# A decoder trunk in split fp32: the seven products of a block in another sequence, and the first six steps as plain fp32

## The chip, the core and the metric

The kernel runs on one core of a Trainium2 chip. Its time is the device time of one execution in microseconds. TensorE (PE) multiplies and writes to PSUM, eight banks of 512 fp32 columns on 128 partitions; weight loads into it have a row of their own (PEld). VectorE (DVE), ScalarE (ACT) and GpSimd (POOL) do the elementwise work; SyncE (SP) and POOL issue the DMAs.

## The reference

A stream of 256 tokens by 1024 goes through two layers. Each has a SwiGLU FFN of half weight, an attention and a second such FFN. The first attention is stick-breaking with 16 heads, the second a sliding window with sinks on shared keys and values. Four FFNs in all make most of the arithmetic:

```
def swiglu(x, w_in, w_out):
    gate, up = jnp.split(x @ w_in, 2, axis=-1)
    return (jax.nn.silu(gate) * up) @ w_out

h = h + 0.5 * swiglu(rms_norm(h, ffn1_norm[layer]), ffn1_w_in[layer], ffn1_w_out[layer])
...
h = h + 0.5 * swiglu(rms_norm(h, ffn2_norm[layer]), ffn2_w_in[layer], ffn2_w_out[layer])
```

with w_in 1024 x 5632 and w_out 2816 x 1024, all fp32.

## The kernel before

**Split products.** A weight comes from HBM as fp32 into one of five `raw` buffers of 1 MB. `split` (L394) makes two operands of the faster type fp32r of it: ACT casts it into `w_hi`, and DVE subtracts that from `raw` into `w_lo`, each in two halves. x is kept split the same way as `xh` and `xl` (both in the tile `xT`). One step of k (`step`, L423) is then three products of 512 columns into one PSUM bank: x_hi by w_hi, x_lo by w_hi, x_hi by w_lo.

**Blocks of an FFN.** The 2816 columns are cut into blocks of 512 (`plain`, "p", or `strassen`, "s") and one of 256 (`narrow`, "h"). The first FFN is p, h, s, s, s, s; the other three are h and five s. A plain block takes both token tiles t by gate and up by 1024 of k, 32 steps. A Strassen block computes the 2 x 2 problem (two tiles by gate and up, the two halves of k) with seven products of four steps in place of eight, in three banks a, d and b (`strassen`, L713). Its raw weights are r11 (gate, first half of k), r12 (up, first half), r22 (up, second half), r21 (gate, second half), and sums of them that DVE makes in place or that POOL adds by DMA. In the order of the code:

1. a: tile 0 by r11; ACT copies a into b (L751), where b goes on from it. In the first Strassen block of the last three FFNs ACT copies a into the SBUF tile s1 instead.
2. d: first operand sum by r11 + r12; ACT copies d into the SBUF tile p5 (`stage`, L735; the profile calls it p).
3. d: fourth operand sum by r22, added to what is in d.
4. b: tile 0 by r21; then silu into s1.
5. a: second operand sum by r11 + r12 + r22 of step 2's buffer; ACT copies a into u2 (the profile's u). DVE then makes s1 * (u2 + d), and PE turns the result (`turn`, L641).
6. a: third operand sum by r12 + r22; DVE adds a to p5.
7. a: tile 1 by r11 + gate's second half; silu, times p5, and a second turn.

Products 3 and 6 write the bank that ACT has just copied, so they wait for that copy. Between 6 and 7 stands the product of the block before with its w_out (`out`).

**What sets the order.** Nothing runs in the order of the code. `Plan` (L118) collects tasks with an engine, an estimated duration and dependencies, and lists them engine by engine with a priority queue: what is ready in its estimate and has the lowest priority goes next. So steps of another product or of `out` are drawn in where a step would wait. Each engine then works its own list strictly in that order. A freed `raw` buffer goes to the back of a queue (`Slots`), and the next load takes the front one and waits for the last reader of it.

**The opening.** x of tile 0 comes in two halves, then the first gate weight in four pieces of 256 KB, x of tile 1, and further weights. PE transposes x (`first_operand`, L1339), DVE multiplies it by the norm's gain in PSUM (L1342), ACT and DVE split it into xh and xl. PE runs warm-up products on a constant until the first split weights are there. Block p takes each half weight for both tiles in turn.

## Time and profile before

| | us |
|---|---|
| median of 3 runs | 913.63 |
| lowest and highest | 913.60, 913.98 |
| the profiled execution | 913.31 |
| its span, first to last instruction | 911.5 |
| PE busy | 899.3 |
| DVE busy | 818.2 |
| ACT busy | 649.6 |

In a timeline row stand start, time taken, engine, line, operation, output and inputs, shapes, the number of merged instructions, and in brackets the engine's idle time before them with what ended it. In a row of stretches stand, for PE, PEld, DVE, ACT and POOL, the busy time with the number of instructions, then the granted PE clock, the DMA engines' mean share and GB/s. A row of waits has the total in us, the number of times and the longest. Ends of products are modelled and overlap, so what a product costs is read from start to start.

### The profile page before, as it was taken

How to read it: one execution, taken by the hardware profiler on the slowest of the kernel's cores; microseconds unless marked ns; L12 is line 12 of the kernel's file. 1: busy time of each engine (PE TensorE's matmuls, PEld its weight loads, DVE VectorE, ACT ScalarE, POOL GpSimd, SP SyncE). 2: the span in 40 equal slices, each digit the busy share in tenths (PEclk: the TensorE clock that was granted, in tenths of full speed). 3: DMA queues.
4: the chain of work that ended last, by engine and by line, in shares of the span. 5: the costliest groups of instructions: out<-in, count | busy, mean ns of one | idle time of the engine just before them, and what ended most of it. 6: DMA issues, size and time to landing. Idle time of an engine off the chain costs nothing.

```text
span 911.5 us, 11855 instructions
## 1 busy us (share of the span) xinstructions
PE 899.3 (99%) x4446; PEld 743.7 (82%) x4446; DVE 818.2 (90%) x981; ACT 649.6 (71%) x925; POOL 65.5 (7%) x71
## 2 busy tenths in 40 slices
PE   9999999999999999999999999999999999999997
PEld 7888888888888878888888878888897777888886
DVE  7989999787967999999969999999689799999986
ACT  6857668677986865876778767667867677686663
POOL 1010101000000100110000101010000001010100
PEclk9999999999999999999999999999999999999999
DMA  9887999996853499999884999899853349998971
GB/s 335 311 203 216 306 268 242 311 246 186 264 184 126 106 260 284 236 280 303 251 269 135 251 279 276 256 326 234 298 180 116 94 94 273 293 258 268 335 209 47
DMA packets 107306, 214.44 MB, mean 235 GB/s; under 512 B 6256, under 2 KB 27760, under 8 KB 107248
## 3 DMA queue, kind: packets, MB, share of 16 engines
q1 hardware_dynamic: 85184, 170.49, 52.3%
q0 software_dynamic: 21648, 42.99, 27.2%
q8 instruction: 35, 0.57, 0.2%
q10 hardware_dynamic: 416, 0.20, 0.1%
q14 instruction: 23, 0.19, 0.1%
HBM read 212.62 MB, written 1.05 MB: 234 GB/s over the span
## 4 chain that ended last, share of the span: by engine, by line
PE 81%; DVE 15%; issue 2%; ACT 2%; POOL 0%; DVEq 0%; POOLq 0%; ACTq 0%
PE ps L283 77%; DVE w_lo L406 6%; PE ps L641 2%; DVE raw L575 1%; PE ps L455 1%; ACT w_hi L404 1%; DVE S_l L545 1%; DVE s L551 1%; DVE xT L462 1%; DVE w_lo L1115 1%; PE ps L1281 0%; DVE xs L1379 0%; DVE hN L532 0%; DVE aT_l L462 0%; DVE e L1273 0%
## 5 line engine op out<-in xcount | busy, mean ns | idle before, releaser
L406 DVE TENSOR_TENSOR w_lo<-raw,w_hi 128x1024 fp32r<-128x1024 f32 x432 | 509.3, 1221 | 30.3 <-ACT w_hi L404 28.5
L404 ACT CAST w_hi<-raw 128x1024 fp32r<-128x1024 f32 x432 | 430.1, 1050 | 96.7 <-DVE raw L575 41.1
L283 PE MATMUL ps<-w_hi,xT 128*128 128x512 f32 (+1 forms) x800 | 233.3, 375 | 0.0
L283 PEld LDWEIGHTS ps<-w_hi,xT 128*128 128x128 f32 x800 | 144.7, 188 | 25.9 <-DVE xT L462 0.2
L283 PE MATMUL ps<-w_lo,xT 128*128 128x512 f32 (+1 forms) x400 | 149.2, 373 | 0.3 <-DVE w_lo L406 0.3
L283 PE MATMUL ps<-w_hi,aT_h 128*128 128x512 f32 x354 | 139.9, 395 | 0.0
L283 PE MATMUL ps<-w_lo,aT_h 128*128 128x512 f32 x354 | 137.7, 389 | 0.0
L283 PE MATMUL ps<-w_hi,aT_l 128*128 128x512 f32 x354 | 137.5, 388 | 0.0
L283 PE MATMUL ps<-w_hi,S_h 128*128 128x512 f32 x320 | 126.9, 396 | 1.5 <-ACT p L735 1.5
L283 PE MATMUL ps<-w_lo,S_h 128*128 128x512 f32 x320 | 124.9, 390 | 0.3 <-DVE w_lo L406 0.3
L283 PE MATMUL ps<-w_hi,S_l 128*128 128x512 f32 x320 | 124.7, 390 | 0.0
L575 DVE TENSOR_TENSOR raw<-raw 128x1024 f32<-128x1024 f32 x78 | 93.7, 1221 | 0.2
L283 PEld LDWEIGHTS ps<-w_lo,xT 128*128 128x128 f32 x400 | 75.3, 188 | 14.4 <-DVE w_lo L406 1.1
L580 POOL DMA_DIRECT2D raw<-in_ffn_w_in_dram x38 | 48.1, 1267 | 516.8 <-DVE w_lo L406 218.0
L283 PEld LDWEIGHTS ps<-w_lo,aT_h 128*128 128x128 f32 x354 | 66.5, 188 | 13.9
L283 PEld LDWEIGHTS ps<-w_hi,aT_l 128*128 128x128 f32 x354 | 66.6, 188 | 12.9
L283 PEld LDWEIGHTS ps<-w_hi,aT_h 128*128 128x128 f32 x354 | 66.5, 188 | 12.8
L283 PEld LDWEIGHTS ps<-w_hi,S_h 128*128 128x128 f32 x320 | 60.1, 188 | 15.3 <-ACT p L735 3.0
L283 PEld LDWEIGHTS ps<-w_lo,S_h 128*128 128x128 f32 x320 | 60.1, 188 | 13.5 <-DVE w_lo L406 0.7
L283 PEld LDWEIGHTS ps<-w_hi,S_l 128*128 128x128 f32 x320 | 60.2, 188 | 11.6
L461 ACT CAST aT_h<-ps 128x512 fp32r<-128x512 f32 (+1 forms) x48 | 26.4, 549 | 55.1 <-PE ps L641 53.6
L283 PE MATMUL ps<-xT,w_hi 128*128 128x512 f32 (+1 forms) x136 | 46.8, 393 | 0.0
(176 smaller groups left out, 918.5 us busy)
## 6 DMA issues: line engine op xcount, KB each, us to landing
raw<-in_ffn_w_in_dram SPq DMA_DIRECT2D x76, 1024.0 KB, 7.8
raw<-in_ffn_w_out_dram SPq DMA_DIRECT2D x44, 1024.0 KB, 6.6
raw<-in_ffn_w_in_dram POOLq DMA_DIRECT2D x38, 1024.0 KB, 9.6
raw<-in_sb_w_qkv_dram SPq DMA_DIRECT2D x12, 1024.0 KB, 9.4
raw<-in_ffn_w_in_dram SPq DMA_DIRECT2D x16, 512.0 KB, 6.7
raw<-in_ffn_w_in_dram SPq DMA_DIRECT2D x16, 256.0 KB, 5.4
raw<-in_sb_w_o_dram SPq DMA_DIRECT2D x4, 1024.0 KB, 5.2
raw<-in_swa_w_q_dram SPq DMA_DIRECT2D x4, 1024.0 KB, 9.3
```

Of the source, the lines that this page charges most:

```text
L283: PE.matmul(ps, lhsT=lhsT, rhs=rhs, start=start, stop=stop, skip_group_check=True)
L404: T("ACT", act(m), lambda sl=sl: ACT.copy(out=flat(hi)[:, sl], in_=flat(raw)[:, sl]), r=[(raw, i) for i in rs] + first, w=[(hi, i) for i i ...
L406: T("DVE", dve(m), lambda sl=sl: DVE.tensor_sub(out=flat(lo)[:, sl], in0=flat(raw)[:, sl], in1=flat(hi)[:, sl].bitcast(F32)), r=[(raw, i) ...
L455: PE.matmul(bank.ap[:, i * P:(i + 1) * P], lhsT=s, rhs=ident, start=i == 0, stop=True, is_transpose=True, skip_group_check=True)
L461: T("ACT", act(n), lambda: ACT.copy(out=hi[2](), in_=src()), r=B(bank), w=[hi[0:2]])
L462: T("DVE", dve(n), lambda: DVE.tensor_sub(out=lo[2](), in0=src(), in1=hi[2]().bitcast(F32)), r=B(bank) + [hi[0:2]], w=[lo[0:2]])
L545: T("DVE", dve(512), lambda: DVE.tensor_sub(out=SL.ap[:, i].rearrange("p a b -> p (a b)"), in0=b.ap, in1=SH.ap[:, i].rearrange("p a b -> p ...
L551: T("DVE", dve(512), lambda: DVE.scalar_tensor_tensor(out=dst.ap, in0=x_.ap, scalar=sign, in1=y_.ap, op0=ALU.mult, op1=ALU.subtract), r=B( ...
L575: T("DVE", dve(m), lambda sl=sl: DVE.tensor_add(out=flat(dst)[:, sl], in0=flat(dst)[:, sl], in1=flat(src)[:, sl]), r=[(src, k) for k in ks ...
L580: T("POOL", 1500, lambda: nc.gpsimd.dma_start(out=dst.ap, in_=src, accum_op=ALU.add), w=[(dst, 0), (dst, 1)], prio=plan.pos - LOADS, lat=5 ...
L641: PE.transpose(out=tr.ap[:, i * P:(i + 1) * P], in_=m.ap[:, i * P:(i + 1) * P], identity=ident)
L1115: T("DVE", dve(512), lambda k=k, g_=g_: DVE.scalar_tensor_tensor(out=lo.ap[:, k], in0=raw.ap[:, k], scalar=g_(), in1=hi.ap[:, k].bitcast(F ...
```

## The change

*The sequence in a Strassen block* (`ORD = "6t"`). Product 3 (`third`) moves behind product 5 and its copy u2. Product 4 (`second`) thereby follows product 2 and its copy p5. In the first Strassen block of the last three FFNs `second` moves further ahead, right behind product 1. The first turn stands ahead of product 6 as before.

*The opening.* For tile 0, the first six of gate's eight steps of k (`DIRECT = 6`) are one product each of unsplit fp32 operands: the raw weight and `x_f`, an SBUF tile into which DVE now writes the multiplied x. xh and xl are made from x_f too, and ACT copies x_f back into the bank. The weights of block p are still split, for tile 1 and the other steps, and now in four quarters each (`FINES`, `split_fine`). Block p now goes tile by tile (`FIRST_T`): gate and up of tile 0, then of tile 1. Warm-up tasks of two products fall from 20 to 10 (`WARM`), and the second tile's x gets a later place (`POSX`).

```diff
+DIRECT = 6
+FINES = (4, 4, 4, 4)
+FIRST_T = True
+ORD = "6t"
-WARM = 14
+WARM = 9
-POSX = (-20000.0, -6000.0)
+POSX = (-20000.0, 0.0)
...
+    def split_fine(raw, prio):
+        a, b = raw.ab
+        hi, lo = WP.get([P, a, b], F32R, "w_hi"), WP.get([P, a, b], F32R, "w_lo")
+        n = a // raw.fine
+        for c in range(0, a, n):
...
+            T("ACT", act(n * b), lambda sl=sl: ACT.copy(out=flat(hi)[:, sl], in_=flat(raw)[:, sl]),
...
+            T("DVE", dve(n * b), lambda sl=sl: DVE.tensor_sub(out=flat(lo)[:, sl], in0=flat(raw)[:, sl],
...
+    def direct(bank, raw, kk, xf, first, last):
+        def run():
+            mm(bank.ap, xf.ap[:, kk], raw.ap[:, kk], first, last)
+
+        dense(4 * 512 / 2.4 + 20, run, r=[(raw, kk), (xf, 0)], w=B(bank))
...
                     for i in range(2):
+                        if first and t == 0 and 4 * i < DIRECT:
+                            raw = load([(slice(0, 512), col(0, i, c))], 4, 512, cut)
+                            gw[i] = split(raw)
+                            for kk in range(4):
+                                if 4 * i + kk < DIRECT:
+                                    direct(b, raw, kk, plainly[i], i == kk == 0, i == 1 and kk == 3)
+                                else:
+                                    step(b, gw[i], kk, of_x(0, 4 * i + kk), i == kk == 0, i == 1 and kk == 3)
+                            RAW.put(raw)
+                            STG.put(plainly[i])
+                            continue
                         gate(t, i, b)
...
+            early = n == 1 and blocks[0] != "p"
+
+            def second(c11):
+                product(b, r21, lambda kk: of_x(0, 4 + kk), not c11, True)
+                RAW.put(r21)
...
+            def third():
+                product(d, r22, of_s(3), False, True)
+                RAW.put(r22)
+
             product(a, r11, lambda kk: of_x(0, kk), True, False)
...
+            if early:
+                second(False)
             add(r11, r12)
             product(d, r11, of_s(0), True, False)
             p5 = stage(d, "p5")
...
-            product(d, r22, of_s(3), False, True)
-            RAW.put(r22)
-            product(b, r21, lambda kk: of_x(0, 4 + kk), not c11, True)
-            RAW.put(r21)
...
+            if not early:
+                second(C11)
...
             product(a, r11, of_s(1), False, False)
             fetch(r11, col(0, 1, c))
             u2 = stage(a, "u2")
+            if ORD[0] == "6":
+                third()
             plus(u2, d)
...
-                outs[n] = plain(n, cols_[n], n == 0 and not first, 4 if first and n == 0 else 2)
+                outs[n] = plain(n, cols_[n], n == 0 and (FIRST_T or not first), 4 if first and n == 0 else 2)
...
+        if t == 0 and 4 * j < DIRECT:
+            plainly[j] = xf = STG.get([P, 4, P], F32, "x_f")
+            T("DVE", dve(512), lambda: DVE.tensor_mul(
+                out=xf.ap, in0=quarters(bank), in1=gin[:, j].unsqueeze(2).to_broadcast([P, 4, P])), r=B(gc, bank), w=B(xf))
...
+            copy_act(lambda: quarters(bank), lambda: xf.ap, 512, B(xf), B(bank), prio=0.0)
+            return
```

On PE, at the start of the program, these rows stood behind the last warm-ups (hN is x, its transposes go to ps; w_hi_178 and w_lo_202 are the first gate weight):

```order
L283 LDWEIGHTS warm_71
L283 MATMUL ps_66<-warm_71 128x256
L455 MATMUL ps_66<-ident_68,hN_63 128x128 x4
L283 MATMUL ps_66<-w_hi_178,xT_158 128x512 x2
L283 MATMUL ps_66<-w_lo_202,xT_158 128x512
L455 MATMUL ps_66<-ident_68,hN_63 128x128 x4
L283 MATMUL ps_66<-w_hi_178,xT_158 128x512 x2
```

And now, from the last of four warm-ups on (raw_113 and raw_185 are the two halves of k of the gate weight, w_hi_170 and w_lo_176 the split of the first):

```order
L288 LDWEIGHTS warm_71
L288 MATMUL ps_66<-warm_71 128x256
L288 MATMUL ps_66<-raw_113,x_f_152 128x512 x4
L491 MATMUL ps_66<-ident_68,hN_63 128x128 x4
L288 LDWEIGHTS warm_71
L288 MATMUL ps_66<-warm_71 128x256
L288 LDWEIGHTS warm_71
L288 MATMUL ps_66<-warm_71 128x256
L491 MATMUL ps_66<-ident_68,hN_63 128x128 x4
L288 MATMUL ps_66<-raw_185,x_f_167 128x512 x2
L288 MATMUL ps_66<-w_hi_170,xT_163 128x512 x2
L288 MATMUL ps_66<-w_lo_176,xT_163 128x512
```

The plain products stand ahead of the second tile's transposes; 22 warm-ups that stood before the first product are gone from there, and three split steps of tile 1 follow the sixth plain product before tile 0's last two steps.

On PE, in the second Strassen block of the third FFN, these rows stood where d's first product (w_hi_4234) ends and d's second (w_hi_4263, the split of r22) begins:

```order
L283 MATMUL ps_66<-w_hi_4234,S_h_4019 128x512
L283 MATMUL ps_66<-w_hi_4234,S_l_4035 128x512
L283 MATMUL ps_66<-w_lo_4251,S_h_4019 128x512
L283 MATMUL ps_66<-w_hi_4263,S_h_4019 128x512
L283 MATMUL ps_66<-w_hi_4263,S_l_4035 128x512
L283 MATMUL ps_66<-w_lo_4280,S_h_4019 128x512
L641 MATMUL ps_66<-ident_68,m_4298 128x128 x4
```

And now (w_hi_4236 is d's first product, w_hi_4268 b's, w_hi_4303 a's second, w_hi_4284 d's second):

```order
L288 MATMUL ps_66<-w_hi_4236,S_h_4025 128x512
L288 MATMUL ps_66<-w_hi_4236,S_l_4032 128x512
L288 MATMUL ps_66<-w_lo_4250,S_h_4025 128x512
L288 MATMUL ps_66<-w_hi_4268,xT_163 128x512 x2
L288 MATMUL ps_66<-w_lo_4282,xT_163 128x512
...
L288 MATMUL ps_66<-w_hi_4303,S_h_4025 128x512
L288 MATMUL ps_66<-w_hi_4303,S_l_4032 128x512
L288 MATMUL ps_66<-w_lo_4319,S_h_4025 128x512
...
L288 MATMUL ps_66<-w_hi_4284,S_h_4025 128x512
```

Four steps of b and two of a stand where nothing stood; steps of a's second and d's second product then alternate by twos.

More of the change, by code (lines that the diff above doesn't have):

```diff
@@ L47 @@
 BOOST = 10000.0
+DIRECT = 6
+FINES = (4, 4, 4, 4)
+AFTER = 4
+FIRST_T = True
 C11 = True
@@ L101, in __init__ @@
         self.slot = None
-        self.by_halves = False
+        self.by_halves = self.fine = False
     @property
@@ L385, in load @@
         raw.ab, raw.cut = (a, b), cut
+        raw.fine, raw.after = 2, {}
+        if cut == 4:
+            raw.fine = FINES[fines[0]]
+            if fines[0] == 0:
+                raw.after = {k: [(xh, (0, 0))] for k in range(AFTER, 4)}
+            fines[0] += 1
         return raw
+    fines = [0]
     def flat(buf):
@@ L395, in split @@
         a, b = raw.ab
+        if raw.cut == 4:
+            return split_fine(raw, prio)
         hi, lo = WP.get([P, a, b], F32R, "w_hi"), WP.get([P, a, b], F32R, "w_lo")
@@ L409, in split @@
         return hi, lo
+    def split_fine(raw, prio):
[3 more added lines that the diff above has]
+        for c in range(0, a, n):
+            ks, at_ = range(c, c + n), [(buf, k) for buf in (hi,) for k in range(c, c + n)]
+            sl = slice(c * b, (c + n) * b)
+            T("ACT", act(n * b), lambda sl=sl: ACT.copy(out=flat(hi)[:, sl], in_=flat(raw)[:, sl]),
+              r=[(raw, k) for k in ks] + raw.after.get(c, []), w=[(hi, k) for k in ks], prio=prio)
+            T("DVE", dve(n * b), lambda sl=sl: DVE.tensor_sub(out=flat(lo)[:, sl], in0=flat(raw)[:, sl],
+                                                              in1=flat(hi)[:, sl].bitcast(F32)),
+              r=[(raw, k) for k in ks] + [(hi, k) for k in ks], w=[(lo, k) for k in ks], prio=prio)
+        hi.fine = lo.fine = True
+        return hi, lo
     def weight(parts, a, b, cut=2, keep=False):
@@ L425, in step @@
         hi, lo = w
-        piece = kk // 2 if piece is None else piece
+        piece = kk if hi.fine else kk // 2 if piece is None else piece
         def run():
@@ L744, in mul_less @@
                   r=r + (B(roots[t][1]) if late else []), w=w, lat=LAT["DVE"] + TM)
+            early = n == 1 and blocks[0] != "p"
+            def second(c11):
+                product(b, r21, lambda kk: of_x(0, 4 + kk), not c11, True)
+                RAW.put(r21)
+                if c11:
+                    silu(lambda: s1.ap, lambda: b.ap, B(b), B(s1), 0)
+                else:
+                    plus(s1, b)
+                    silu(lambda: s1.ap, lambda: s1.ap, [], B(s1), 0)
+            def third():
+                product(d, r22, of_s(3), False, True)
+                RAW.put(r22)
             product(a, r11, lambda kk: of_x(0, kk), True, False)
-            c11 = C11 and (n != 1 or blocks[0] == "p" or C11_0)
-            if c11:
+            if C11 and not early:
                 T("ACT", act(512), lambda: ACT.copy(out=b.ap, in_=a.ap), r=B(a), w=B(b), prio=plan.pos - STAGE)
@@ L765, in strassen @@
                 add(r12, r22)
-            product(d, r22, of_s(3), False, True)
-            RAW.put(r22)
-            product(b, r21, lambda kk: of_x(0, 4 + kk), not c11, True)
-            RAW.put(r21)
-            if c11:
-                silu(lambda: s1.ap, lambda: b.ap, B(b), B(s1), 0)
-            else:
-                plus(s1, b)
-                silu(lambda: s1.ap, lambda: s1.ap, [], B(s1), 0)
+            if ORD[0] == "3":
+                third()
+            if not early:
+                second(C11)
+            if ORD[0] == "2":
+                third()
             product(a, r11, of_s(1), False, False)
@@ L777, in strassen @@
             u2 = stage(a, "u2")
+            if ORD[0] == "6":
+                third()
             plus(u2, d)
@@ L780, in strassen @@
             STG.put(u2)
-            turn(s1, 0, aT)
+            if ORD[1] == "t":
+                turn(s1, 0, aT)
             product(a, r12, of_s(2), False, False)
@@ L784, in strassen @@
             plus(p5, a)
+            if ORD[1] != "t":
+                turn(s1, 0, aT)
             between()
@@ L1337 @@
     T("ACT", 60, lambda: nc.scalar.dma_start(out=gin, in_=ffn1_norm[0].rearrange("(j p k) -> p j k", j=2, k=4)), w=B(gc), prio=-9.5e5, lat=2500.0)
+    plainly = {}
     def first_operand(t, j, bank):
         transposes(bank, lambda: [hN.ap[:, t, half(j)].rearrange("p (q k) -> p k q", k=4)[:, k, :] for k in range(4)], [(hN, (t, j))])
+        if t == 0 and 4 * j < DIRECT:
+            plainly[j] = xf = STG.get([P, 4, P], F32, "x_f")
+            T("DVE", dve(512), lambda: DVE.tensor_mul(
+                out=xf.ap, in0=quarters(bank), in1=gin[:, j].unsqueeze(2).to_broadcast([P, 4, P])), r=B(gc, bank), w=B(xf))
+            T("ACT", act(512), lambda: ACT.copy(out=xh.ap[:, 4 * j:4 * j + 4, ts(t)], in_=xf.ap), r=B(xf), w=[(xh, (t, j))])
+            T("DVE", dve(512), lambda: DVE.tensor_sub(out=xl.ap[:, 4 * j:4 * j + 4, ts(t)], in0=xf.ap, in1=xh.ap[:, 4 * j:4 * j + 4, ts(t)].bitcast(F32)),
+              r=B(xf) + [(xh, (t, j))], w=[(xl, (t, j))])
+            copy_act(lambda: quarters(bank), lambda: xf.ap, 512, B(xf), B(bank), prio=0.0)
+            return
         T("DVE", dve(512), lambda: DVE.tensor_mul(
```

## The prediction

> **What bounds the kernel now.** I read the page first, then a table by stretches, then the waits, then the timeline at each place where TensorE (PE) stood still.
>
> ```profile
> PE 899.3 (99%) x4446; PEld 743.7 (82%) x4446; DVE 818.2 (90%) x981; ACT 649.6 (71%) x925; POOL 65.5 (7%) x71
> PE 81%; DVE 15%; issue 2%; ACT 2%; POOL 0%; DVEq 0%; POOLq 0%; ACTq 0%
> 50.00:70.00 20.00, 20.00 (x90) 16.56 (x89) 15.96 (x16) 12.26 (x15) 1.20 (x1) 1.00 0.96 254
> 9.50:32.50 23.00, 23.00 (x108) 19.05 (x107) 18.96 (x23) 16.69 (x22) 0.55 (x1) 1.00 1.06 384
> 300.00:400.00 100.00, 99.78 (x449) 81.39 (x449) 97.06 (x104) 71.55 (x92) 10.39 (x8) 1.00 0.87 245
> 500.00:600.00 100.00, 99.17 (x447) 81.31 (x446) 97.75 (x98) 71.93 (x86) 8.92 (x7) 1.00 0.92 266
> ```
>
> PE bounds it: 99% busy, 81% of the chain, full granted clock. In the stretch 50 to 70 us PE never stands, and a product of 512 columns starts every 0.227 us (the timeline rows below: 525.53, 525.76, 525.99). So there are two ways to gain: less PE work, or fewer places at which PE stands. VectorE (DVE) is next: 97 to 98% busy in the stretches of the second and third FFN. Where does PE stand? Among the waits, those on lines that the change touches are few:
>
> ```profile
> PEld ps L283 <- ACT p L735: 3.0, 4, 1.1
> PEld ps L283 <- DVE w_lo L406: 2.1, 4, 0.7
> PEld ps L283 <- ACT u L735: 0.6, 2, 0.4
> ```
>
> The rows say that weight loads waited 4 times for the ScalarE copy into p and twice for the one into u: 6 times in 19 blocks with two copies each. In the other 32 cases the order already puts other steps between. The timeline shows what a wait costs PE:
>
> ```profile
> 525.53 0.39 PE L283 MATMUL ps<-w_hi,S_h 128*128 128x512 f32 x1
> 525.76 0.39 PE L283 MATMUL ps<-w_hi,S_l 128*128 128x512 f32 x1
> 525.99 0.39 PE L283 MATMUL ps<-w_lo,S_h 128*128 128x512 f32 x1
> 527.05 0.50 PE L283 MATMUL ps<-w_hi,S_h 128*128 128x512 f32 x1 [0.68 <-ACT p L735]
> 527.39 0.39 PE L283 MATMUL ps<-w_hi,S_l 128*128 128x512 f32 x1
> 526.41 0.59 ACT L735 COPY p<-ps 128x512 f32<-128x512 f32 x1 [1.22 <-PE ps L283]
> 773.76 0.39 PE L283 MATMUL ps<-w_lo,S_h 128*128 128x512 f32 x1
> 775.16 0.39 PE L283 MATMUL ps<-w_hi,S_l 128*128 128x512 f32 x1
> 501.82 0.39 PE L283 MATMUL ps<-w_lo,xT 128*128 128x512 f32 x1
> 502.70 0.40 PE L283 MATMUL ps<-w_hi,S_l 128*128 128x512 f32 x1
> 350.21 0.39 PE L283 MATMUL ps<-w_lo,aT_h 128*128 128x512 f32 x1
> 350.94 0.40 PE L283 MATMUL ps<-w_hi,S_l 128*128 128x512 f32 x1
> ```
>
> The last product of bank d starts at 525.99; two products on, undisturbed, would be 526.44, and it is 527.39: 0.95 us lost. The same sum, second product after the wait less the one before it less 0.454, gives 0.95 at 774, 0.43 at 502 and 0.28 at 350. These four make 2.61 us. The other two waits are small, or stand behind a late w_lo.
>
> **The change part by part.** *Order of the products.* It adds no instruction to a block. The copy of d into p takes 0.59 us and the whole round from d's last product to its next one 1.06 us (525.99 to 527.05). Before, half a product (6 instructions, 1.4 us) stood in between at most, and nothing at the two places of 0.95 us. The changed order puts b's whole product there and 2 to 4 steps of a: 18 or more instructions, 4.1 us. Between a's copy u and a's next product it puts d's second product (at one block half of it, the other half stands ahead). Cover of 1.4 to 4.1 us against a need of about 1.1: all four waits should go, **-2.6 us**. Bounds: 0, if PE stands at the same places for w_lo instead, and -3.6, the sum of both rows on p and u. I take nearly all, since the cover is up to four times the need. What is late next is the turn of tile 0: it needs d's second product, an addition and a multiplication on DVE (0.75 us each at most, the row at 399.77 below), and has a's third product (2.7 us) as cover.
>
> *The opening.* Now:
>
> ```profile
> 4.96 1.06 PE L455 MATMUL ps<-ident,hN 128*128 128x128 f32 x4
> 5.82 3.46 PE L283 MATMUL ps<-warm 128*128 128x256 bf16 x26
> 9.12 0.64 PE L455 MATMUL ps<-ident,hN 128*128 128x128 f32 x4
> 9.52 0.70 PE L283 MATMUL ps<-w_hi,xT 128*128 128x512 f32 x2
> 31.70 0.40 PE L283 MATMUL ps<-w_lo,xT 128*128 128x512 f32 x1
> 4.78 0.70 DVE L1342 TENSOR_TENSOR ps<-ps,gcols 128x512 f32<-128x512 f32 x1 [1.68 <-PE ps L455]
> 6.67 0.68 DVE L462 TENSOR_TENSOR xT<-ps,xT 128x512 fp32r<-128x512 f32 x1
> 8.61 2.36 DVE L406 TENSOR_TENSOR w_lo<-raw,w_hi 128x1024 fp32r<-128x1024 f32 x2
> 23.98 2.36 DVE L406 TENSOR_TENSOR w_lo<-raw,w_hi 128x1024 fp32r<-128x1024 f32 x2 [2.51 <-ACT w_hi L404]
> raw<-in_ffn_w_in_dram SPq DMA_DIRECT2D x16, 256.0 KB, 5.4
> 240.53 1.52 PE L283 MATMUL ps<-e,v 128*64 128x256 f32 x16
> ```
>
> PE fills up to 9.5 us with 26 warm-up products, since the split of the first weights and of x is not done; the 96 products of block p then run from 9.52 to 31.70. After the change four warm-ups follow the second transposes and then the plain products. x_f is the result of the multiplication that starts at 4.78 and takes 0.70, so it is there at 5.5; the first quarter weights are issued from 1.65 us on and land 5.4 us after issue at the most of the 16, the first ones sooner. I take PE's own queue as what sets the start: four warm-ups at the slow spacing from 5.82 (the transposes beside them take 1.06 for four, later 0.64) end near 6.7.
>
> A plain fp32 product does not occur at 512 columns. Its price by the nearest row: 16 records in 1.52 us at 240.53, which are 8 instructions of two records each, run as pairs on two column halves, 4 of 256 and 4 of 128 columns: 2 x (2 x 256 + 2 x 128) = 1536 columns one after another, less the 0.16 us by which each modelled product outlasts its spacing: 0.885 ns a column, so 2 x 512 columns cost 0.9 us. Bounds: 0.44, if it went like a transpose (four of 128 columns at the full clock, about 0.11 each), and 0.91, four products of 0.227. I take 0.9, the row of a true fp32 product. It replaces 3 x 0.227 = 0.68, so six cost 1.3 us more PE work.
>
> Sum from 6.7: six direct 5.4, two groups of four transposes 0.9, two warm-ups 0.2, 77 split products to the start of the last 17.5: 30.7, against 31.70. **-1.0 us**; by the bounds of the price -1.0 to -3.8, but the queue on DVE does not allow the latter, and it can also cost: up to k7's low part DVE has four passes over x of tile 0, four of tile 1 and eight quarter pieces of weights, 16 x 0.65 (0.68 a piece, a little overlapped) from 4.8 us: 15.2 to 15.9. PE asks for it after 6.7 + 5.4 + 1.1 + three steps of the second tile 2.0 + 0.7 = 15.9, and would wait up to 0.7. So -0.3 to -1.5.
>
> Tile 0 first (by_t) makes PE take a quarter weight each 0.68 us in the first pass where both tiles shared it before. Block p's 256 KB at 384 GB/s (row 9.50) land every 0.68 us: just in time, hidden while PE starts up no earlier than computed. The finer split costs DVE 4 x 0.68 - 2.36 = 0.4 us a weight, 1.6 in all; the 2.5 us that DVE stood before 23.98 hide it, and if they were used up, it would come back on PE as a w_lo wait of that size. POOL and the DMAs of later blocks move with PE.
>
> *Sum.* 913.31 (the profiled execution's own time; span 911.5) - 2.6 - 1.0 = 909.7. The median of the runs shown stands 0.3 higher, so I predict **910.0 us**.
>
> **The rivals.** *DVE takes over.* DVE is 97 to 98% busy where the four waits are, and the weight loads already waited 2.1 us for w_lo there. If each copy's wait turns into a wait for w_lo, only the opening is left: 913.6 - 1.0 = 912.6. For it: those busy shares. Against it: 2.2 to 2.9 us of DVE are idle in each 100 us, and PE gains but 1 us in each.
>
> *The opening gains nothing*, the order does: 913.6 - 2.6 = 911.0. It needs the w_lo wait above and a late weight. One form of it is the clock. The four transposes of 1.06 and 0.64 us show that the clock rose between 5 and 9 us; before, 26 warm-ups lay over that point, now plain products do. Were it to rise 3.4 us later, 3.4 us of work would run at half rate, 1.7 us lost, and the opening would cost 0.7: 911.7. The Trainium skill ("TensorE: Matmul & The Clock Gate", Part 1) says of this that the throttle's windows of about 3.4 us run free, so that the point varies from run to run; by that rule the loss above would come in some executions. Up to 6.7 us the changed kernel issues the same PE work, and the three times shown (913.6 to 913.98) show no such spread, so I give it little.
>
> *Slower: the third product holds its weight too long.* r22's raw buffer is freed by its split, now after the split for a's second product; the next block's first weight waits for it on SP.
>
> ```profile
> 375.25 10.98 SPq L364 DMA_DIRECT2D raw<-in_ffn_w_in_dram  x4
> 382.98 2.00 ACT L404 CAST w_hi<-raw 128x1024 fp32r<-128x1024 f32 x2 [0.38 <-DMA raw<-in_ffn_w_in_dram]
> 395.23 4.63 DVE L406 TENSOR_TENSOR w_lo<-raw,w_hi 128x1024 fp32r<-128x1024 f32 x4
> 399.77 0.75 DVE L742 SCALAR_TENSOR_TENSOR m<-p,small,m 128x512 f32<-128x512 f32 x1
> 397.15 0.62 PE L283 MATMUL ps<-w_hi,xT 128*128 128x512 f32 x2
> ```
>
> That load was issued at 375.25 and its split began at 382.98 the moment it landed; the next block's first product started at 397.15. Four pieces of w_lo (4.63) stand between the old and the new release, so the split starts near 387.6, and its four passes on two engines end by about 391: 6 us early. But DVE works in a fixed order and has 3 us spare in 100. If it stands 0.6 us in each of the 12 blocks behind another block in FFNs two to four, that is 7.2 us: 913.6 + 7.2 - 3.6 = 917. It decides from about 4 us of delay beyond these 6, or where DVE's spare time is used up.
>
> **How the numbers follow.** Forecast (order and opening both gain) 0.58; DVE takes over 0.16; the opening gains nothing 0.12; a late weight makes it slower 0.07; more than forecast (w_lo waits go too, 908) 0.07. A measurement of this kernel tells about 0.2%, 1.8 us, from no change: below 911.8 is faster, above 915.5 slower. Faster: 0.58 + 0.07 + most of 0.12 = 0.74; the same: 0.16 and the rest, 0.20; slower 0.06. Range 907.8 to 913.2: it takes in both one-sided cases and leaves out the slow one and the far gain.
>
> **What would show it.** Right: the waits for p and u gone from the list; direct products from 6.7 us, two records of about 0.45 each; the last split product of block p near 30.7 (31.1 where the first turn stands ahead of it). DVE takes over: the w_lo wait grows from 2.1 to about 5. Late weights: ScalarE's idle time before w_hi from DMA grows, and PE's share falls below 98% in the stretches above. Clock: the first direct products last about 0.9 a record. I am wrong if PE's gain in 300 to 600 us is not there without any w_lo wait in its place.

## The result, and the profile after

| | before | after |
|---|---|---|
| median, us | 913.81 | 926.69 |
| lowest to highest | 913.60 to 914.89 | 924.50 to 929.73 |
| the profiled execution | 913.31 | 924.50 |
| its span | 911.5 | 922.7 |

The ratio is 1.0141, with a 95% interval of 1.0111 to 1.0171: slower by 1.4%. The forecast was 910.0, faster, with a range to 913.2. Direction and range are both wrong.

On the page of the changed kernel, the row of busy times and the first row of the chain read now:

```profile
PE 905.2 (98%) x4420; PEld 739.5 (80%) x4420; DVE 816.6 (89%) x989; ACT 646.3 (70%) x935; POOL 66.8 (7%) x71
...
PE 41%; DVE 24%; DMA 19%; issue 10%; ACT 6%; POOL 0%; ACTq 0%; POOLq 0%; DVEq 0%; SPq 0%
```

The chain was 81% PE before. Now it runs through PE for 41% only, through DVE for 24 and through DMAs for 19, nearly all of them w_in loads (18). DVE is less busy than before (89% against 90), in a longer time: it is not short of time, it stands and waits. Two stretches before:

```profile
400.00:500.00 100.00, 100.00 (x467) 82.90 (x466) 90.69 (x110) 74.63 (x107) 7.07 (x6) 1.00 0.81 239
800.00:900.00 100.00, 100.00 (x457) 82.83 (x456) 90.88 (x95) 66.69 (x81) 7.02 (x6) 1.00 0.82 235
```

And the stretches after:

```profile
300.00:400.00 100.00, 99.19 (x441) 79.67 (x440) 92.03 (x99) 65.42 (x83) 9.30 (x8) 1.00 0.87 242
400.00:500.00 100.00, 98.04 (x448) 78.74 (x447) 90.30 (x108) 72.92 (x104) 7.49 (x7) 1.00 0.83 238
500.00:600.00 100.00, 99.46 (x449) 81.46 (x448) 97.14 (x99) 73.43 (x91) 8.92 (x7) 1.00 0.92 257
800.00:900.00 100.00, 97.44 (x435) 78.52 (x434) 87.82 (x87) 63.72 (x76) 7.65 (x6) 1.00 0.91 260
```

From 300 to 400 us DVE fell from 97.06 to 92.03 us. PE stands in the second and fourth FFN, and gains 0.3 us in the stretch of the third where the two copies into p had cost it. The waits say for what; the first row is from before, the others from after:

```profile
ACT w_hi L404 <- DMA raw<-in_ffn_w_in_dram: 30.0, 15, 4.2
...
ACT w_hi L419 <- DMA raw<-in_ffn_w_in_dram: 69.8, 22, 7.7
...
DVE w_lo L421 <- ACT w_hi L419: 51.7, 29, 4.2
...
PEld ps L288 <- DVE w_lo L421: 11.3, 19, 1.0
...
PEld ps L677 <- DVE m L789: 4.8, 5, 1.5
...
PEld ps L288 <- ACT w_hi L419: 3.6, 5, 1.7
...
PEld ps L288 <- ACT u L782: 0.5, 1, 0.5
```

The waits for p are gone, and that for u stands once. In their place PE waits 19 times for w_lo (2.1 us before, 4 times), for w_hi (0.2 before) and for m ahead of a turn (0.3 before). Behind all three stand the first two rows: ScalarE waited 30.0 us for w_in loads before, 69.8 now.

Where along the program? Four of ScalarE's instructions are easy to find again in both traces: a table load near the end of the first attention, v_s (the shared values, made between the second and the third FFN), a table load behind the third FFN, and the first scaling of the output. Before:

```profile
280.77 1.28 ACT L1073 ACT_TABLE_LOAD   x1
...
478.77 0.51 ACT L1148 ACTIVATE v_s<-ps,small 128x256 f32<-128x256 f32 x1
...
645.43 1.28 ACT L1172 ACT_TABLE_LOAD   x1
...
900.75 0.62 ACT L1490 ACTIVATE hg<-hg,small 128x384 f32<-128x384 f32 x1 [1.36 <-DVE hg L1479]
```

After:

```profile
280.17 1.28 ACT L1138 ACT_TABLE_LOAD   x1
...
483.77 0.47 ACT L1213 ACTIVATE v_s<-ps,small 128x256 f32<-128x256 f32 x1
...
651.65 1.28 ACT L1237 ACT_TABLE_LOAD   x1
...
911.38 0.62 ACT L1566 ACTIVATE hg<-hg,small 128x384 f32<-128x384 f32 x1 [1.36 <-DVE hg L1555]
```

The changed kernel is 0.6 us ahead after the first FFN and attention (the opening's gain less two waits of the first FFN), 5.0 behind after the second FFN, 6.2 after the third and 10.6 after the fourth.

**One inner block, closely.** The second FFN's block from 375 to 397 us is the one whose rows the prediction showed. A row does not say which weight a load or a split belongs to; the kernel's own lists do, laid in order on the rows of the trace. After, the two loads that matter (SP's row holds four of them, of which 378.45 is the next block's first weight r11; POOL's is the fetch that adds gate's second half for product 7), then DVE and ScalarE:

```profile
378.45 9.68 SPq L369 DMA_DIRECT2D raw<-in_ffn_w_in_dram  x4
...
377.61 1.28 POOL L616 DMA_DIRECT2D raw<-in_ffn_w_in_dram  x1 [9.33 <-DMA raw<-in_ffn_w_out_dram]
...
374.90 4.62 DVE L421 TENSOR_TENSOR w_lo<-raw,w_hi 128x1024 fp32r<-128x1024 f32 x4
...
392.50 4.63 DVE L421 TENSOR_TENSOR w_lo<-raw,w_hi 128x1024 fp32r<-128x1024 f32 x4 [4.12 <-ACT w_hi L419]
...
391.42 3.90 ACT L419 CAST w_hi<-raw 128x1024 fp32r<-128x1024 f32 x4 [4.67 <-DMA raw<-in_ffn_w_in_dram]
```

And before:

```profile
378.00 1.27 POOL L580 DMA_DIRECT2D raw<-in_ffn_w_in_dram  x1 [11.06 <-DVE w_lo L406]
...
387.49 1.22 DVE L406 TENSOR_TENSOR w_lo<-raw,w_hi 128x1024 fp32r<-128x1024 f32 x1
...
390.55 2.36 DVE L406 TENSOR_TENSOR w_lo<-raw,w_hi 128x1024 fp32r<-128x1024 f32 x2 [1.25 <-ACT w_hi L404]
...
389.46 2.00 ACT L404 CAST w_hi<-raw 128x1024 fp32r<-128x1024 f32 x2 [3.14 <-DMA raw<-in_ffn_w_in_dram]
```

DVE's four pieces at 374.90 are r22, product 5's weight, r22 and a first half of a w_out weight: product 5's weight and r22 are split half by half in turn. The third piece, r22's second half, ends at 378.38 and frees r22's buffer, and SP issues the next block's r11 at 378.45, against 375.25. It now goes out 0.8 us behind the fetch, where it went 2.8 us ahead of it. The issues of these two DMAs with size and time to landing, after:

```profile
raw<-in_ffn_w_in_dram POOLq DMA_DIRECT2D x1, 1024.0 KB, 13.7
raw<-in_ffn_w_in_dram SPq DMA_DIRECT2D x1, 1024.0 KB, 10.0
```

Before:

```profile
raw<-in_ffn_w_in_dram SPq DMA_DIRECT2D x1, 1024.0 KB, 7.7
raw<-in_ffn_w_in_dram POOLq DMA_DIRECT2D x1, 1024.0 KB, 11.4
```

Both take 2.3 us longer. Over the 19 Strassen blocks the fetch of product 7's weight took 10.6 us at the median before and 12.7 after. Over the 15 blocks that another Strassen block follows in the same FFN, the next r11 landed 1.8 us after product 5's weight was split at the median before, and 10.7 us after it now. And the lists differ. Before, the second half of r11's split (387.49) filled DVE's wait for the fetched weight. In the changed kernel's lists the next r11 comes behind the fetched weight (DVE's row at 392.50 holds two pieces of the one, then two of the other), so DVE stands 4.12 us there, against 1.25.

### The profile page after: what moved, and what is told of

Same layout as the page of the kernel before. It is cut to its first block, busy times and chain, and to the rows that moved or that the text cites. A ratio compares the mean times of both kernels' runs of the same rounds, so it can differ in the third digit from the quotient of the medians.

```text
span 922.7 us, 11848 instructions
## 1 busy us (share of the span) xinstructions
PE 905.2 (98%) x4420; PEld 739.5 (80%) x4420; DVE 816.6 (89%) x989; ACT 646.3 (70%) x935; POOL 66.8 (7%) x71
## 4 chain that ended last, share of the span: by engine, by line
PE 41%; DVE 24%; DMA 19%; issue 10%; ACT 6%; POOL 0%; ACTq 0%; POOLq 0%; DVEq 0%; SPq 0%
PE ps L288 38%; DMA raw<-in_ffn_w_in_dram 18%; DVE w_lo L421 15%; ACT w_hi L419 5%; DVE raw L611 4%; PE ps L491 1%; DVE aT_l L498 1%; PE ps L677 1%; PE ps L1346 1%; DMA raw<-in_ffn_w_out_dram 1%; DVE s L587 0%; DVE S_l L581 0%; DVE u L786 0%; DVE xT L498 0%; DVE p L786 0%
## 5 line engine op out<-in xcount | busy, mean ns | idle before, releaser
L421 DVE TENSOR_TENSOR w_lo<-raw,w_hi 128x1024 fp32r<-128x1024 f32 x424 | 498.3, 1217 | 52.9 <-ACT w_hi L419 51.7
L419 ACT CAST w_hi<-raw 128x1024 fp32r<-128x1024 f32 x424 | 424.4, 1050 | 141.5 <-DMA raw<-in_ffn_w_in_dram 69.8
L288 PEld LDWEIGHTS ps<-w_hi,aT_l 128*128 128x128 f32 x354 | 66.6, 188 | 12.9
```

Of the source, the lines that this page charges most:

```text
L288: PE.matmul(ps, lhsT=lhsT, rhs=rhs, start=start, stop=stop, skip_group_check=True)
L419: T("ACT", act(m), lambda sl=sl: ACT.copy(out=flat(hi)[:, sl], in_=flat(raw)[:, sl]), r=[(raw, i) for i in rs] + first, w=[(hi, i) for i i ...
L421: T("DVE", dve(m), lambda sl=sl: DVE.tensor_sub(out=flat(lo)[:, sl], in0=flat(raw)[:, sl], in1=flat(hi)[:, sl].bitcast(F32)), r=[(raw, i) ...
```

## The experiments

Fifteen kernels, each timed in several executions beside the kernel before on the same chip. *Inner* blocks are those 15 with a product with w_out between product 6 and product 7; the last Strassen block of each FFN has none.

| | ratio to before | interval |
|---|---|---|
| the change | 1.0141 | 1.0111 to 1.0171 |
| opening_only | 0.9979 | 0.9969 to 0.9989 |
| order_only | 1.0122 | 1.0107 to 1.0137 |
| other_slot | 1.0074 | 1.0059 to 1.0089 |
| early_split | 1.0015 | 1.0002 to 1.0027 |
| early_inner | 0.9979 | 0.9970 to 0.9989 |
| last_old | 1.0086 | 1.0067 to 1.0105 |
| late_load | 1.0045 | 1.0030 to 1.0059 |
| third_after_second | 0.9975 | 0.9966 to 0.9985 |
| slot_inner | 1.0066 | 1.0049 to 1.0082 |
| first_ffn_old | 0.9977 | 0.9968 to 0.9986 |
| no_early_second | 0.9978 | 0.9969 to 0.9986 |
| held_buffer | 1.0009 | 0.9995 to 1.0024 |
| fill | 1.0082 | 1.0053 to 1.0112 |
| nofill | 1.0189 | 1.0168 to 1.0211 |
| nofill_early | 1.0006 | 0.9997 to 1.0015 |

### Which part of the change: opening_only and order_only

The first is the change with `strassen` as it was; the second sets the opening back:

```diff
-DIRECT = 6
+DIRECT = 0
-FIRST_T = True
+FIRST_T = False
-WARM = 9
+WARM = 14
-POSX = (-20000.0, 0.0)
+POSX = (-20000.0, -6000.0)
...
-        if raw.cut == 4:
-            return split_fine(raw, prio)
```

> The opening alone; in every Strassen block the products stand in the sequence of before. Theory A (the third product behind the fifth holds r22's raw buffer longer, so the next block's first load starts later): the loss belongs to the sequence alone, and the opening keeps the 1.8 us that the two timelines show at the start of the narrow block: 913.8 - 1.8 = 912.0. Rival B (the opening shifts all that follows against the DMAs, and the late weights come from there): above 920.

> The new sequence of the products alone, with the opening of before. Theory A: the time of the change without the opening's gain, 926.7 + 1.8 = 928.5, with ScalarE's idle time before w_hi from the DMA near 70 us. Rival B (opening as the cause): no slower than before, near 911.

Measured: 912.62 and 925.47 us, beside 914.38 for the kernel before. The opening gains 0.2%, as theory A said. The sequence of the products alone is slower by 1.2%, 11 us, where 928.5 us was expected, and ScalarE waits 70.3 us for w_in loads in its trace. Rival B falls.

### The buffer or the sequence: other_slot and early_split

In both, r22's split is called ahead of product 4. In other_slot only the queue of free buffers changes by it: in 13 of the 15 inner blocks DVE still splits r22 behind product 5's first half. In early_split the sum r11 + r22 has to wait for r22's low part, which puts the split back to its old place in all of them, and with it the moment at which r22's buffer comes free:

```diff
             def third():
-                product(d, r22, of_s(3), False, True)
-                RAW.put(r22)
+                product(d, r22, of_s(3), False, True, w22)
...
+            w22 = split(r22)
+            RAW.put(r22)
             if not early:
                 second(C11)
```

```diff
-                product(d, r22, of_s(3), False, True)
+                product(d, r22, of_s(3), False, True, w22)
...
-                add(r11, r22)
+                w22 = split(r22)
+                add(r11, r22, [(w22[1], 0), (w22[1], 1)])
```

> The change, but r22's raw buffer is handed back in the queue of free buffers ahead of r21's, as before, so that the next block's r11 takes the buffer of r21, which is free early, and a w_out weight takes the late one. Product sequence as in the change. Theory A: the first load of the next block starts as early as before, so most of the 11 to 13 us go; the w_out load is 3 to 4 us later instead: 910 to 915. Rival C (not the buffer but the sequence itself: the turn of tile 0 right behind product 3 waits for DVE, and the splits are wanted in another sequence): still above 920.

> The change, but r22 is split right after product 2's weight, ahead of the sum r11 + r22, as DVE did before; products in the sequence of the change, the split operands of r22 just wait longer. Theory A: r22's buffer is free as early as before, DVE's idle time before the fetched r11 falls from 4.1 to about 1.2 us in a block, the waits on p and u stay gone: 913.8 - 1.8 - 2.6 = 909.4 (907 to 912). Rival C (the sequence itself): above 920, with the turns still waiting for m.

Measured: 921.21 and 915.56. With the products in the changed sequence, putting r22's split back takes away 11 of the 13 us: the sequence on PE is not what costs (rival C falls), the place of one split is, with what hangs on it. Handing the next r11 another buffer takes away half, though its load is then not late at all: it lands 0.7 us after product 5's split at the median (10.7 in the change, 1.8 before). So theory A was right in direction but too simple. In other_slot the w_out weight is the late one, and early_split is still 3 us above opening_only. Its trace shows most of that in one place, the last block of the first FFN, where no product with w_out stands ahead of product 7:

```profile
162.90 0.73 PE L288 MATMUL ps<-w_hi,xT 128*128 128x512 f32 x2 [2.58 <-ACT w_hi L419]
164.16 0.79 PE L288 MATMUL ps<-w_lo,xT 128*128 128x512 f32 x1 [0.53 <-DVE w_lo L421]
```

That weight's fetch was issued at 147.39 and took 14.4 us.

### Last blocks and inner blocks: early_inner and last_old

Both give the last Strassen block of each FFN the old sequence, early_inner on early_split, last_old on the change:

```diff
+            behind = ORD[0] == "6" and n < last
+            if not behind:
+                third()
...
-            if ORD[0] == "6":
+            if behind:
                 third()
```

> As early_split, but the last block of each FFN, which has no product with w_out between product 6 and product 7, keeps the sequence of before. In early_split PE stood 2.85 and 1.09 us there at 163 us, with half-rate products behind, since product 7's weight landed 14.4 us after its issue. Theory A2 (late r22 in the inner blocks, late last weight in the last ones, nothing else): that stall goes, and with the opening's 1.8 and the four waits' 2.6 us: 913.8 - 1.8 - 2.6 = 909.4 (908 to 911.5). Rival C (the new sequence costs by itself): no better than 914.

> The change, with the last block of each FFN in the sequence of before; in the inner blocks r22 is split late as in the change. Theory A2: of the 13 us only the stalls in the last blocks go (0.7 at 163, 1.6 at 457, 3.8 with the half-rate products at 646 to 650, 1.0 at 900: about 7), and the inner blocks' remain: 918 to 921. If the last blocks were all of it: 912.

Measured: 912.22 and 921.93. From 1.0141 to 1.0086, 5.0 us of the loss stood in the last blocks (7 expected). That share is the change's own: from early_split to early_inner the same edit gives 3.3 us. From 1.0086 to 0.9979, 9.8 us stood in the inner blocks, and all of it goes with r22's split. One row of the table by stretches, for the same stretch of the second FFN, shows it. The kernel before:

```profile
320.00:460.00 140.00, 139.78 (x631) 114.65 (x630) 131.48 (x131) 94.18 (x112) 10.20 (x8) 1.00 0.94 271
```

The change:

```profile
320.00:460.00 140.00, 137.23 (x607) 108.97 (x606) 125.04 (x126) 90.31 (x107) 10.20 (x8) 1.00 0.90 253
```

early_inner:

```profile
320.00:460.00 140.00, 140.00 (x633) 115.04 (x632) 130.15 (x129) 94.97 (x112) 10.20 (x8) 1.00 0.94 265
```

In 140 us DVE gets 6.4 us less done in the change than before, and PE 24 instructions fewer; last_old is nearly the same (126.41 us and 612 instructions). With the early split PE has 633 of them and never stands. But early_inner was to be 909.4, and it is no faster than opening_only. The four waits of 2.6 us are gone and the gain is not there. Its trace shows what took their place, in the fourth FFN above all: product 7's weight in the last block once more (0.2 and 0.5 us of standing at 886 and 887), and the copy of a into b (L812), which product 4 now follows sooner:

```profile
772.96 0.72 PE L288 MATMUL ps<-w_hi,xT 128*128 128x512 f32 x2 [0.70 <-ACT ps L812]
```

### The suspected cause, in part: late_load; and a smaller step: third_after_second

late_load is the kernel before, in whose plan the buffer that the next block's r11 takes is busy until product 5's weight is split:

```diff
             product(a, r11, of_s(1), False, False)
+            r21.all.append([t for t in r11.all if t.eng == "DVE"][-1])
             fetch(r11, col(0, 1, c))
```

third_after_second is the change with product 3 right behind product 4, so that r22 is split ahead of product 5's weight:

```diff
-ORD = "6t"
+ORD = "2t"
```

> The kernel before, with one thing added: the next block's first load waits until the weight of product 5 is split, 2 to 3 us later than it does now; products, splits and opening as before. Theory A: the late load alone makes the loss: DVE's idle time before the next block's first split grows by about 2 us in the 12 inner blocks of FFNs two to four, some of which PE loses: 916 to 922. Rival C (the sequence of products and splits): 914, no change.

> The change, with product 3 right behind product 4 (ahead of product 5): the copy p still has all of product 4 (2.7 us) as cover, and r22 is split ahead of product 5's weight as before. Theory A: little or no late load, p's waits gone, u's (0.6) back: 909 to 912. Rival C: slower by the share of the sequence that is kept, 918 or more.

Measured: 917.63 and 912.39. late_load is slower than the kernel before by 0.45%, some of it in the last block of the fourth FFN. But it does not hold the load as far as was meant. The added dependency counts in the planner's estimates alone, and SP waits for what really reads the buffer: in all 15 inner blocks of the trace r11's load still goes out before product 5's weight is split, 2.9 us at the median, against 3.5 before. It lands 4.3 us after that split, where it was 1.8 before and 10.7 in the change. So the run shows a cost with a part of the lateness, in other lists. And with product 3 one place later than before, but not two, the loss is gone, with 0.9975 in place of 1.0141. p keeps product 4 as cover there, and r22's split stays early in 12 of the 15 inner blocks. That it gains nothing over the opening alone is the same miss as in early_inner.

### Two mixtures: first_ffn_old and no_early_second

first_ffn_old is early_split with the old sequence in the first FFN's last block only; no_early_second is the same with product 4 of the first Strassen blocks behind product 2 again:

```diff
+            behind = ORD[0] == "6" and not (first and n == last)
+            if not behind:
+                third()
```

```diff
-            early = n == 1 and blocks[0] != "p"
+            early = False
```

> As early_split, but only the last block of the first FFN keeps the sequence of before (early_split's stall of 2.85 and 1.09 us with half-rate products stood there; its later FFNs ran 1.2 us faster than before). If the traces of early_split and early_inner add up: 914.1 - 1.1 at the end of the first attention - 1.2 later = 911.7, a little faster than the opening alone (912.4). If the gain from the waits on p and u is spent elsewhere: 912.3, as the opening alone.

> As first_ffn_old, but in the first Strassen block of the last three FFNs product 4 stays behind product 2 and is not moved right behind product 1. It tells what this third part of the new sequence does: 911.7 if nothing; 1 us more if it is what took p's wait there (0.43 us at 502 and 0.2 at 750 in the trace of before).

Measured: 911.71 and 912.10, ratios of 0.9977 and 0.9978. Neither can be told from opening_only (0.9979). The early place of product 4 does nothing that can be measured, and the opening is all the gain there is. These, opening_only, early_inner and third_after_second are the kernels that beat both the one before and the change, by 0.2% against the one before.

### What it is in the inner blocks: slot_inner, held_buffer, fill, nofill, nofill_early

slot_inner is other_slot with the old last blocks. held_buffer is early_inner, in whose plan r22's buffer is handed on only when product 5's weight is split:

```diff
             product(a, r11, of_s(1), False, False)
+            if behind:
+                r22.all.append([t for t in r11.all if t.eng == "DVE"][-1])
             fetch(r11, col(0, 1, c))
```

The other three force the sequence of two splits in ScalarE's and DVE's lists: in fill (on last_old) product 7's fetched weight behind the next block's r11, as before; in nofill (on held_buffer) and nofill_early (on early_inner) the other way round (`fetched` holds the tasks of the fetched weight's split). These are dependencies within one engine's list, and the traces have them as meant: r11 stands first in all 15 inner blocks of fill and in none of the other two:

```diff
+            at_ = len(plan.tasks)
+            w1 = split(r11)
+            for t_ in plan.tasks[at_:]:
+                for f in fetched:
+                    if f.eng == t_.eng:
+                        f.deps.add(t_)
-            product(a, r11, lambda kk: of_x(0, kk), True, False)
+            product(a, r11, lambda kk: of_x(0, kk), True, False, w1)
```

> As other_slot (the next block's first load takes r21's buffer, free early; r22 is still split behind product 5's weight), with the last block of each FFN in the sequence of before, as in last_old (1.0086). It tells apart, in the inner blocks, the late load from the late split of r22. If the late load is all: as early_inner, 912 to 913. If the place of r22's split costs by itself (turns and products that wait for DVE): 918 to 921, little better than last_old.

> As early_inner (0.9979: r22 split early in the inner blocks, last blocks as before), with one thing added: in the inner blocks r22's buffer is handed on only when the weight of product 5 is split too, the same point in DVE's work at which the change hands it on. Sequence of products and of the splits of r22 and product 5's weight stay those of early_inner. If the late hand-over is the loss of the inner blocks: as last_old (1.0086), 919 to 922. If the place of r22's split costs: as early_inner, 912 to 913. The addition of the late load to the kernel before cost 0.45%, part of it at its last block, so a share of 0.2 to 0.5% from the buffer alone, 914 to 917, would leave the rest to the place of the split.

> last_old, with one thing changed: the split of product 7's fetched weight has to come after the split of the next block's first weight on ScalarE and DVE, as in the kernel before. Theory F (the loss of the inner blocks is DVE standing for the fetched weight with nothing to fill the wait): DVE's idle time from 320 to 460 us falls from 13.6 to about 9 us and most of the 9.8 us go: 913 to 916. Rival G (the late split of r22 and the turns that wait for m): still 919 to 922.

> held_buffer (1.0009), with the split of the next block's first weight forced behind the split of product 7's fetched weight. Theory F: late buffer and this sequence together make the whole loss, though r22 is split early: 1.006 to 1.009, 919 to 922. Rival G: no change, 914 to 916.

> early_inner (0.9979) with the same forced sequence, the buffer handed on early. Theory F: DVE stands about 2.4 us longer in a block, in 12 blocks, of which PE loses what DVE's spare time does not take up: 916 to 920. Rival G: 912 to 913.

Measured: 920.39, 915.17, 920.51, 931.75 and 914.70.

*slot_inner* is the run that takes the late r11 away and leaves the late split. Its next r11 lands 0.8 us after product 5's split at the median, earlier than before, and ScalarE waits 37.6 us for w_in loads, against 62.4 in last_old. Yet the time is 1.0066, against 1.0086, and the two intervals overlap. So with the lateness moved from the next r11 to a w_out weight, some 2 of the 9.8 us of the inner blocks go and about 8 stay; r22 is split late in 13 of them still. (In other_slot, with the new last blocks, the same edit took 6 us: the shares do not add up.)

*held_buffer* was to be its counterpart, an early split with a late r11, and it is not. As in late_load, the added dependency moves the planner's lists and not the wait on the chip. In the block of the second FFN that was shown, SP issues the next r11 at 371.20, while the third of these pieces of DVE, which ends product 5's split, runs up to 374.58:

```profile
371.20 0.37 SPq L369 DMA_DIRECT2D raw<-in_ffn_w_in_dram  x1
...
371.09 3.49 DVE L421 TENSOR_TENSOR w_lo<-raw,w_hi 128x1024 fp32r<-128x1024 f32 x3
...
ACT w_hi L419 <- DMA raw<-in_ffn_w_in_dram: 27.7, 14, 4.4
```

So it is in all 15 inner blocks, by 3.7 us at the median, as in early_inner, and ScalarE waits 27.7 us for w_in loads, less than in early_inner (32.4). What held_buffer loses against early_inner, 0.30%, is therefore not the price of a late buffer; it comes with another list.

*nofill_early and nofill.* Against early_inner (0.9979) the forced sequence of the two splits costs 0.27% in nofill_early. Together with held_buffer's edit it costs 2.1% in nofill, nearly four times the sum of the two and more than the whole change, without a load that is really held: the next r11 lands 3.2 us after product 5's split at the median. There PE waits 19.8 us for w_lo. So the planner's lists alone can move the time by 2%.

*fill* missed: theory F said 913 to 916, and it stays where last_old was. Over the inner blocks DVE stands 2.5 us for the fetched weight, 20.8 in last_old, but 22.3 us for the next r11, 5.6 in last_old. With a late r11 the forced sequence only moves the standing from one weight to the other, so the run decides neither for theory F nor against it. Its trace has as long a wait for m as the change, and new ones for p, the long ones in last blocks, which have the old sequence:

```profile
PEld ps L677 <- DVE m L789: 4.8, 5, 1.7
...
PEld ps L288 <- ACT p L782: 4.4, 3, 2.0
```

**What is shown and what stays open.** Shown: the loss belongs to the sequence of products; 5.0 us of it go when the last blocks get the old sequence; the other 9.8 go when r22 alone is split at its old place; and of these 9.8 some 8 are still there when the next r11 comes in time. Open: how the rest divides between r22's late split itself, the w_out weight that gets its buffer late, the two lists and the turns behind the late split. No run has a late r11 and nothing else: late_load has a part of it, held_buffer none. Each edit also gives the planner another list, and fill and nofill show how far that alone can move a loss.

## Why the prediction was wrong, point by point

**The four waits of 2.6 us: right in mechanism, wrong as a gain.** They are gone, and the cover was long enough. But early_inner and third_after_second, in which r22 is split early and the loss is gone, are no faster than the opening alone.

**The step that failed** is the term for the order of the products: -2.6 us, with bounds of 0 to -3.6. It put the cost of splitting and releasing r22 later at nothing. The runs show +11 us for the order alone (order_only, 1.0122), of which none is left with r22 split early and the old last blocks (early_inner, 0.9979). The late release stood among the rivals, as "Slower: the third product holds its weight too long" with a chance of 0.07, and there it was priced as if everything else stood still. It put the next r11's split near 387.6 and its four passes' end at 391, 6 us early. In the trace that split runs on DVE as the last two pieces of the row at 392.50, which ends at 397.13. Three things were not counted. The load and the fetch, issued 0.8 us apart, each took 2.3 us longer. The split now stands behind the fetched weight's in both lists. And DVE, which "has 3 us spare in 100", stood 2.9 us longer in this one block (4.12 less 1.25), so its spare time was gone and everything behind it came late: product 5's and 6's weights, and m. That the rival's 7.2 us for 12 blocks is not far from the 9.8 that the inner ones lost is luck: its 0.6 us a block was assumed, and by slot_inner most of the loss is there without the late load that it told of.

**What was missed altogether** are the last blocks. Product 7's weight is fetched once product 5's is split, and lands 8 to 14 us later. In an inner block PE has a product with w_out in between; in the last one it has none. In the four last blocks the fetch took 10.3 to 12.5 us before and 12.9 to 14.4 after, and product 7 waited for it in all four after and in none before. They cost 5.0 us by last_old.

**The turn.** The one named as late next, of tile 0, never waited for its multiplication. It is the turn of tile 1, which waits for m on a late DVE: 4.8 us on the weight load, 0.3 before.

**The rival "DVE takes over"** came true in form. w_lo waits went from 2.1 to 11.3 us. But it was priced as the loss of a gain, not as a loss.

**The opening: right, mis-sized.** Its rows after:

```profile
5.51 0.61 PE L288 MATMUL ps<-warm 128*128 128x256 bf16 x4
...
5.95 3.60 PE L288 MATMUL ps<-raw,x_f 128*128 128x512 f32 x8
...
10.55 1.88 PE L288 MATMUL ps<-raw,x_f 128*128 128x512 f32 x4
...
30.34 0.39 PE L288 MATMUL ps<-w_lo,xT 128*128 128x512 f32 x1
```

Twelve records for six products, 3.60 us for eight: less the 0.17 by which a modelled end outlasts the spacing, 0.43 a record and 0.86 a product (0.9 said). The granted clock is 1.00 from 5.95 to 12 us. They start at 5.95, not at 6.7: the four warm-ups in front begin 0.3 us sooner than assumed and run at 0.11 each (0.44 us in all), not at the slow spacing. The last split product of block p starts at 30.34, with the first turn now ahead of it: 1.4 us earlier than 31.70 plus 0.36 for that turn, 1.7 in all against 1.0 forecast. opening_only confirms it with 0.2%. The wait for k7's low part did not come, nor did the clock rise late: with 0.43 us from the first record to the last at that granted clock, there is no half rate in them.

**What would show it.** The list was of use in part: ScalarE's idle time before w_hi from the DMA grew as the late weight was said to make it, and w_lo's wait passed the 5 us of its rival. PE's share did not fall below 98% in the stretches named there (99.2 and 99.5%), only from 800 to 900 us (97.4%). The error was in the price and the chance more than in the signs.

## What to carry to other kernels

In a kernel whose buffers are handed on in a ring, moving a product also moves the moment at which its buffer comes free, and so a load, what that load collides with, and what fills the next wait. Price a step's release as carefully as its work, and look at the stage's end, where what usually lies in between is missing. Small losses do not simply add up: two edits to the plan that cost 0.3% each cost 2.1% together. If a product has to move, its operand's preparation can stay where it was. And before a run that delays one thing is read, look in its trace whether that thing was delayed: a dependency that only the planner knows changes the lists and not the waits.

## What the runs showed of the hardware

**The clock fell after short waits.** In the last block of the third FFN PE waited twice for product 7's weight, and then ran at half rate for a while:

```profile
645.50 0.73 PE L288 MATMUL ps<-w_hi,xT 128*128 128x512 f32 x2 [1.25 <-ACT w_hi L419]
646.76 0.77 PE L288 MATMUL ps<-w_lo,xT 128*128 128x512 f32 x1 [0.53 <-DVE w_lo L421]
647.33 1.06 PE L288 MATMUL ps<-w_hi,xT 128*128 128x512 f32 x2
648.18 0.63 PE L288 MATMUL ps<-w_lo,xT 128*128 128x512 f32 x1
```

From 647.33 to 648.18 there are two products, 0.43 us each where 0.227 is usual, and five more of that kind follow, up to 650.28: 1.4 us lost beside the waits. The row of the stretch has the granted clock, half for 3.41 us:

```profile
646.81:650.22 3.41, 3.41 (x8) 2.76 (x9) 3.30 (x3) 1.47 (x2) 0.00 (x0) 0.50 0.29 83
```

In order_only the same waits were longer, 2.48 and 0.52 us, and behind them the clock stayed full:

```profile
650.61:653.00 2.39, 2.39 (x10) 1.99 (x11) 2.39 (x3) 1.54 (x2) 0.00 (x0) 1.00 0.09 12
```

Pairs of waits of this kind were followed by the half rate in the change, other_slot, early_split and late_load, and not in order_only and slot_inner. The Trainium skill ("TensorE: Matmul & The Clock Gate", Part 1) says that the clock falls after at least one idle window of about 3.4 us, and that these windows run free. The first does not agree with the trace: PE stood 1.25 and 0.53 us here, 1.8 of the 3.41 us before the fall. The second agrees: in each of the four traces the half rate lasts 3.413 us, and from the clock's rise near the start to this fall it is a whole number of such stretches (188 in the change from 5.11 us on; 47, 47 and 261 in other_slot, early_split and late_load). So it can depend on where in a stretch the waits fall; which share of it has to be idle no run shows. It would also make the times spread, and those of the change do, over 5.2 us against 1.3 before, with the lowest mean granted clock (0.995) in the longest execution; that this is the reason wasn't tested.

**An adding fetch is slow.** The 1 MB loads of w_in in the trace of before, through SP and, where they add to what is in the buffer, through POOL, with the median time to landing:

```profile
raw<-in_ffn_w_in_dram SPq DMA_DIRECT2D x76, 1024.0 KB, 7.8
...
raw<-in_ffn_w_in_dram POOLq DMA_DIRECT2D x38, 1024.0 KB, 9.6
```

The adding ones took from 8.3 to 12.5 us before and up to 14.4 after. Product 7's alone, 19 of the 38, took 10.6 us at the median before, 12.7 after, and 9.3 in early_inner. That the next block's load right beside it is what lengthens it fits the block shown above (11.4 and 13.7 us), but no run changes that alone.
